# A Griffin-style block on one Trainium2 core: seven-product gate steps from output block 2 instead of 3

## The chip, the core and the metric

The kernel runs on 1 core of one Trainium2 chip. The metric is the device time of one execution in microseconds (us). Before the change it was 700.57 us, the median of 3 runs (700.04 to 700.89). The engines are called PE (TensorE matmul), PEld (its weight load), DVE (VectorE), ACT (ScalarE), POOL (GpSimd) and SP (SyncE, which here only issues DMAs).

## The reference, cut to what matters

One trunk layer over 512 positions of width 1024, in float32:

```python
h = rms_norm(x, norm_mix_g[l])
proj = h @ w_in[l]                      # conv B | conv C | conv in | q | k | v | forget | gates
y_conv = (cb * causal_dwconv(cc * cin, conv_mix_w[l])) @ w_out_conv[l]
o = forgetting_attention(q, k, v, log_f)
y_attn = o @ w_out_attn[l]
gates = jax.nn.sigmoid(g_logit + b_gate[l])
g_conv, g_attn = jnp.split(gates, 2, axis=-1)
x = x + (g_conv * y_conv + g_attn * y_attn) @ w_o[l]
...
x = x + (jax.nn.silu(a) * b) @ w_down[l]
return rms_norm(x, norm_f_g)
```

The change touches how the two gate projections (`g_logit`, 2048 columns of `proj`) are computed.

## The kernel before, in words

The activations lie transposed: 128 features on the partitions, 8 blocks of features (`KB`), 512 positions along the free axis. A float32 product is made of three passes: each weight chunk and each activation is split into a rounded high part and a low remainder, and `mm3` issues high times high, low times high and high times low, each as two matmuls of 128x256 (L290).

**The weight stream.** `stream` lists the weight chunks in the order of their use. `load` has SP fetch them up to seven chunks ahead into a ring of four buffers (`raw`); `split` then makes the high part on ACT (L259, `wh_...`) and the low part on DVE (L263, `wl_...`). There are only two `wh` and two `wl` buffers, so the high part of a chunk waits until PE is done with the chunk two places earlier. ACT and DVE each work through one fixed list of instructions in order.

**The gate and mix stage** follows the attention and runs over the output blocks j = 0 to 7. For each j it needs two gate projections (`ga`, `gb`), then the chunk `mix{j}` for the two branch outputs `yc` and `ya` (24 matmuls each), and then the merge: L946 and L947 multiply on DVE, L948 adds on POOL, L949 and L950 split the result into `mh` and `ml`. The gate projections come in two kinds:

- Plain (j = 1 and 2; those of j = 0 are done within the attention): chunks `in{20+j}` and `in{28+j}`, 48 matmuls of 128x256 each into `p_ga` and `p_gb`, evacuated by L825 on DVE and L826 on ACT.
- Steps of seven products (j = 3 to 7, `GATES`, function `seven`): a 2x2 block product (two gate columns, two feature blocks 2q and 2q+1, two halves of the positions) is made of seven products instead of eight. A step has a chunk `P{n}` (3 products of each 2x2 block) and a chunk `F{n}` (4 products of each), and covers two values of q, so that a j takes two steps: P, F, P, F, 84 matmuls on four PSUM banks named `dn`, issued by `passes` (L308). `gate_pair` combines them on ACT and DVE.

**What the steps need besides.** The `F` chunks are sums of weights, made in device memory during the attention by DMAs (`make_forms`: SP puts at L198, POOL adds at L201, in groups of two steps, one group per j). The activations need sums too. After the attention's tiles are free POOL fetches x again into `xt` (L834, four DMAs of 512 KB, one for each q). Then, for q = 0, 1 and again for q = 2, 3: ACT scales by the norm gain (L841, two instructions for each q), DVE makes four sums (L849, L850, L853, L854, each over both q), and for each q ACT makes the high part (L860, `xth`) and DVE the low part (L861, `xtl`).

**What sets the order there.** These pieces stand in the list `later`, each with the first chunk at whose split it may be put into the instruction stream and a cost in us. `run_later` puts in those that fit a budget at each split (3.0 for an `in` or `mix` chunk, 1.6 for `P`, 0.75 for `F`); `flush` puts in the rest just ahead of the products that want them.

Of the kernel before, what the change touches and what calls it, by code (L numbers as in the profile page):

```python
# [52 lines left out]
)  # L53
HELD = 2

GJ = 3
GATES = tuple(((j, q), (j, q + 1)) for j in range(GJ, KB) for q in (0, 2))

PLAIN = [(m, k) for m in (6, 7) for k in range(*PHASES[1])]
# [7 lines left out]
def block_kernel(ctx, tc, xT, vecs, wv, win, wmix, wo, wup, wst, wdp, outT):  # L67
# [13 lines left out]
    def bank(i, name):  # L81
        return ps.tile([P, S], F32, tag=f"b{i}", name=name)

    def ring(*ids):
        st = [0]

        def f(name):
            st[0] += 1
            return bank(ids[(st[0] - 1) % len(ids)], name)

        return f
# [29 lines left out]
    stream = [(f"v{kb}", wv[kb], S + H) for kb in range(KB)]  # L121
# [3 lines left out]
    def step_chunks(n):  # L125
        m = len(DOUBLES[n])
        return [(f"P{n}", wst[n, :, : 3 * m * P], 3 * m * P), (f"F{n}", n, 4 * m * P)]

    for j in range(KB):
        if j >= GJ:  # L130
            stream += step_chunks(n) + step_chunks(n + 1)
# [139 lines left out]
    def chunk(name, hl=None):  # L271

        k = chunk.n
        chunk.n += 1
        assert stream[k][0] == name
        if len(parts) == k:
            split(hl)
        return parts[k]
# [3 lines left out]
    def mm3(out, wh, wl, xh, xl, start, stop):  # L282


        n = out.shape[-1]
        cut = [slice(a, a + 2 * P) for a in range(0, n, 2 * P)] if n > 2 * P else [slice(0, n)]
        trio = ((wh, xh), (wl, xh), (wh, xl))
        for i, (w, x) in enumerate(trio):
            for c, cs in enumerate(cut):
                keep(nc.tensor.matmul(  # L290
                    out[:, cs], w, x[:, cs],
                    start=start and i == 0 and c == 0,
                    stop=stop and i == 2 and c == len(cut) - 1,
                ))
# [185 lines left out]
    def proj(idx, name, evac, bank):  # L480
        st = {}

        def half(i):
            if i == 0:
                st["w"] = chunk(f"in{idx}")
                st["p"] = bank(f"p_{name}")
            wh, wl = st["w"]
            for kb in range(4 * i, 4 * i + 4):
                ks = slice(kb * P, (kb + 1) * P)
                mm3(st["p"], wh[:, ks], wl[:, ks], xgh[:, kb, :], xgl[:, kb, :], kb == 0, kb == KB - 1)  # L490
            if i == 1:

                while len(parts) < chunk.n + 2:
                    split()
                with after_split():
                    evac(st["p"])

        return [lambda: half(0), lambda: half(1)]
# [151 lines left out]
    def run_all(fs):  # L650
        for f in fs:
            f()
# [71 lines left out]
    acc, bank_s, bank_t = ring(2, 0, 1), ring(3, 4), ring(5, 6)  # L724
# [43 lines left out]
    def seven(doubles, n0, sets, operand, goes_on=None, stays=None, done=None):  # L768


        todo, wants = [], {}
        for n, d in enumerate(doubles):
            for kind in "PF":
                prods = []
                for s_, (i, q) in enumerate(d):
                    for f, g, b, h in PROD:
                        if (f < 3) == (kind == "P"):
                            wants.setdefault(f"{kind}{n0 + n}", []).append(("q", q))
                            c = 3 * s_ + f if f < 3 else s_ + len(d) * (f - 3)
                            prods.append((c, i, operand(q, g), b, h))  # L780
                todo.append((f"{kind}{n0 + n}", prods))
        users = [{(i, b) for _, i, _, b, _ in prods} for _, prods in todo]
        for n, (name, prods) in enumerate(todo):
            wh, wl = chunk(name)
            flush(wants[name])
            before = set().union(*users[:n])
            after = set().union(*users[n + 1 :])
            out = []
            for c, i, (xh, xl), b, h in prods:
                if i not in open_:  # L790
                    flush(sets[i])
                    open_[i] = [bank(x, f"dn{n0}{i}{x}") for x in sets[i]]
                cs = slice(c * P, (c + 1) * P)
                out.append((
                    open_[i][b][:, th[h]], (i, b), wh[:, cs], wl[:, cs], xh, xl,
                    (i, b) not in before and i != goes_on, (i, b) not in after and i != stays,
                ))
            passes(out, len(out))
            if name[0] == "F":
                for i in sorted({i for _, i, *_ in prods}):  # L800
                    if (i, 0) not in after and i != stays:
                        done(i, open_.pop(i), sets[i])
            split_next()


    acc = ring(3, 4, 5, 6, 0, 1, 2, 7)
    xp = ctx.enter_context(tc.tile_pool(name="xp", bufs=1, side="right"))
    xt = xp.tile([P, KB, S], F32, tag="x1", name="xt")
    xth = xp.tile([P, KB, S], F32R, tag="x1h", name="xth")
# [12 lines left out]
    def evac_gate(idx, dst):  # L822
        def f(p):
            g = mt(f"g{idx}")
            nc.vector.tensor_mul(g, p, rb1)  # L825
            nc.scalar.activation(g, g, AF.Sigmoid, bias=col(BG + idx))  # L826
            dst.append(g)

        return f
# [32 lines left out]

        return f

    k = [c[0] for c in stream].index("mix1")
    for q in (0, 2):
        f, g = x_sums(slice(q, q + 2))
        for i in (q, q + 1):
# [14 lines left out]
    def gate_pair(j, gs):  # L883


        def done(i, banks, ids):
            p23, p45, p16, p7 = banks[0], banks[1], banks[2], banks[3][:, th[0]]
            t = {}

            def z1():  # L890
                t["z"] = mt(f"gz{j}")
                nc.scalar.activation(t["z"][:, th[0]], p16[:, th[0]], AF.Copy)
                nc.vector.tensor_add(t["z"][:, th[1]], p16[:, th[1]], t["z"][:, th[0]])

            def m1():
                gs.append(mt(f"ga{j}"))
                nc.vector.tensor_add(gs[0], p23, t["z"])

            def u3():
                t["u"] = mt(f"gu{j}")[:, : 2 * P]  # L900
                nc.vector.tensor_add(t["u"], p7, t["z"][:, th[1]])
                nc.vector.tensor_add(gs[0][:, th[1]], p45[:, th[1]], gs[0][:, th[1]])

            def m2():
                gs.append(mt(f"gb{j}"))
                nc.vector.tensor_add(
                    gs[1].rearrange(halves_of, h=2), p45.rearrange(halves_of, h=2),
                    t["u"].unsqueeze(1).to_broadcast([P, 2, 2 * P]),
                )

            def fin(n):
                def f():
                    g = gs[n]
                    nc.vector.tensor_mul(g, g, rb1)
                    nc.scalar.activation(g, g, AF.Sigmoid, bias=col(BG + 8 * n + j), scale=(1.0, -1.0)[n])

                return f

            for f, us, x in ((z1, 0.42, 2), (m1, 0.7, 0), (u3, 0.85, 3), (m2, 0.7, 1), (fin(0), 0.7, None), (fin(1), 0.7, None)):
                later.append((0, us, () if x is None else (ids[x],), f))  # L920

        return done

    for j in range(KB):
        gs = []
        if j == 0:
            evac_gate(0, gs)(gp[0])
            evac_gate(8, gs)(gp[1])
        elif j < GJ:
            run_all(proj(20 + j, f"ga{j}", evac_gate(j, gs), acc))  # L930
            run_all(proj(28 + j, f"gb{j}", evac_gate(8 + j, gs), acc))
        else:
            if j == GJ:
                acc = ring(2, 7, 3, 4)
            seven(GATES[2 * (j - GJ) : 2 * (j - GJ) + 2], 2 * (j - GJ), {j: (0, 1, 5, 6)}, gate_form, done=gate_pair(j, gs))
        wh, wl = chunk(f"mix{j}")
        yc, ya = acc(f"yc{j}"), acc(f"ya{j}")
        for pp, hh, ll, o in ((yc, ych, ycl, 0), (ya, oth, otl, 4)):
            for k in range(4):
                ks = slice((o + k) * P, (o + k + 1) * P)  # L940
                mm3(pp, wh[:, ks], wl[:, ks], hh[:, k, :], ll[:, k, :], k == 0, k == 3)
        if j >= GJ:
            split_next()
            flush()
        a, b = gs
        nc.vector.tensor_mul(a, a, yc)  # L946
        nc.vector.tensor_mul(b, b, ya)  # L947
        nc.gpsimd.tensor_add(a, a, b)  # L948
        nc.scalar.activation(mh[:, j, :], a, AF.Copy)  # L949
        nc.vector.tensor_sub(ml[:, j, :], a, mh.bitcast(F32)[:, j, :])  # L950
# [6 lines left out]
    acc = ring(0, 1, 5, 6, 3, 4, 2, 7)  # L957
# [76 lines left out]
    acc = ring(*range(6))  # L1034
# [113 lines left out]
    for ph, (j0, j1) in enumerate(PHASES):  # L1148
        if ph:
            flush()  # L1150
            acc = ring(*X)
# [212 lines left out]
```

## Time and profile before

| | |
|---|---|
| median of 3 runs | 700.57 us (700.04 to 700.89) |
| the profiled execution's own time | 700.14 us |
| span of the profile, first to last instruction | 697.9 us |
| PE busy | 689.5 us (99%) |
| DVE, ACT, POOL busy | 501.1, 344.4, 173.3 us (72%, 49%, 25%) |
| granted TensorE clock, mean | 0.997 |

The profile shows one execution. Times within it count from the span's start. A row of the timeline gives the start, the duration and in brackets the idle time of the engine before the row and who ended it; rows of the same line that follow each other are merged and counted (x4). A PE matmul's end is modelled and overlaps the next one, so a matmul's price is read from the distance between starts, or from the chain of waits, which lays pieces end to end.

### The profile page before, as it was taken

How to read it: one execution, taken by the hardware profiler on the slowest of the kernel's cores; microseconds unless marked ns; L12 is line 12 of the kernel's file. 1: busy time of each engine (PE TensorE's matmuls, PEld its weight loads, DVE VectorE, ACT ScalarE, POOL GpSimd, SP SyncE). 2: the span in 40 equal slices, each digit the busy share in tenths (PEclk: the TensorE clock that was granted, in tenths of full speed). 3: DMA queues.
4: the chain of work that ended last, by engine and by line, in shares of the span. 5: the costliest groups of instructions: out<-in, count | busy, mean ns of one | idle time of the engine just before them, and what ended most of it. 6: DMA issues, size and time to landing. Idle time of an engine off the chain costs nothing.

```text
span 697.9 us, 14608 instructions
## 1 busy us (share of the span) xinstructions
PE 689.5 (99%) x6008; PEld 688.1 (99%) x6008; DVE 501.1 (72%) x783; ACT 344.4 (49%) x546; POOL 173.3 (25%) x191
## 2 busy tenths in 40 slices
PE   9999999999999999999999999999999999999996
PEld 9999999999999999999999999999999999999995
DVE  6677877776677778754377777778674677878793
ACT  5665655545565444543344444445443344445563
POOL 4134847432200000224504214010000313221001
PEclk9999999999999999999999999999999999999998
DMA  7528989542452555587977855555647696776513
GB/s 254 161 72 274 188 196 206 116 93 86 159 165 81 177 190 177 179 301 149 216 194 168 211 130 128 151 170 166 203 126 231 139 196 157 186 169 178 153 31 121
DMA packets 52690, 116.02 MB, mean 166 GB/s; under 512 B 4960, under 2 KB 23408, under 8 KB 52624
## 3 DMA queue, kind: packets, MB, share of 16 engines
q1 hardware_dynamic: 37464, 94.17, 41.9%
q0 software_dynamic: 13920, 19.74, 17.8%
q10 hardware_dynamic: 1240, 1.19, 0.5%
q8 instruction: 47, 0.77, 0.4%
q14 instruction: 19, 0.16, 0.1%
HBM read 112.92 MB, written 33.03 MB: 209 GB/s over the span
## 4 chain that ended last, share of the span: by engine, by line
PE 97%; DMA 1%; DVE 0%; SPq 0%; ACT 0%; issue 0%; DVEq 0%; ACTq 0%
PE p_up L290 26%; PE dn L308 20%; PE p_in L290 14%; PE p_up L308 8%; PE p_wo L290 6%; PE yc L290 3%; PE ya L290 3%; PE p_q L290 2%; PE p_k L290 2%; PE p_gb L290 2%; PE p_ga L290 2%; PE o L635 2%; PE pa L454 2%; PE pb L456 1%; PE tp L618 1%; PE pdB L290 1%
## 5 line engine op out<-in xcount | busy, mean ns | idle before, releaser
L290 PE MATMUL p_up<-x1h,wl_up 128*128 128x256 f32 x536 | 104.5, 276 | 0.0
L290 PE MATMUL p_up<-x1h,wh_up 128*128 128x256 f32 x536 | 104.4, 276 | 0.0
L290 PE MATMUL p_up<-x1l,wh_up 128*128 128x256 f32 x536 | 104.4, 276 | 0.0
L259 ACT ACTIVATE wh_up<-raw_up 128x1024 fp32r<-128x1024 f32 x44 | 46.7, 1060 | 86.8 <-PE p_up L290 73.4
L290 PEld LDWEIGHTS p_up<-x1h,wl_up 128*128 128x128 f32 x536 | 80.8, 188 | 0.0
L290 PEld LDWEIGHTS p_up<-x1l,wh_up 128*128 128x128 f32 x536 | 80.7, 188 | 0.0
L290 PEld LDWEIGHTS p_up<-x1h,wh_up 128*128 128x128 f32 x536 | 80.6, 188 | 0.0
L263 DVE TENSOR_TENSOR wl_up<-raw_up,wh_up 128x1024 fp32r<-128x1024 f32 x44 | 53.8, 1223 | 20.6 <-ACT wh_up L259 20.6
L1061 POOL TENSOR_TENSOR ge<-fu,fu 128x512 f32<-128x512 f32 x11 | 17.1, 1552 | 161.6 <-DVE fu L547 150.8
L290 PE MATMUL p_in<-xgh,wh_in 128*128 128x256 f32 x288 | 56.8, 279 | 0.0
L290 PE MATMUL p_in<-xgh,wl_in 128*128 128x256 f32 x288 | 56.6, 278 | 0.0
L290 PE MATMUL p_in<-xgl,wh_in 128*128 128x256 f32 x288 | 56.5, 278 | 0.0
L201 POOL DMA_DIRECT2D f<-in_wst_dram x48 | 56.1, 1285 | 0.0
L1046 DVE TENSOR_TENSOR fz<-p_up,rb_n 128x512 f32<-128x512 f32 x44 | 30.3, 690 | 31.6 <-PE p_up L290 31.5
L263 DVE TENSOR_TENSOR wl_F<-raw_F,wh_F 128x1024 fp32r<-128x1024 f32 (+1 forms) x30 | 40.4, 1345 | 12.9 <-ACT wh_F L259 12.8
L290 PEld LDWEIGHTS p_in<-xgh,wh_in 128*128 128x128 f32 x288 | 44.7, 188 | 0.7
L259 ACT ACTIVATE wh_F<-raw_F 128x1024 fp32r<-128x1024 f32 (+1 forms) x30 | 31.5, 1051 | 27.6 <-PE dn L308 24.6
L290 PEld LDWEIGHTS p_in<-xgl,wh_in 128*128 128x128 f32 x288 | 43.7, 188 | 0.0
L290 PEld LDWEIGHTS p_in<-xgh,wl_in 128*128 128x128 f32 x288 | 43.6, 188 | 0.0
L308 PE MATMUL p_up<-x1h,wh_up 128*128 128x256 f32 x168 | 40.3, 277 | 0.0
L308 PE MATMUL p_up<-x1l,wh_up 128*128 128x256 f32 x168 | 40.2, 276 | 0.0
L263 DVE TENSOR_TENSOR wl_in<-raw_in,wh_in 128x1024 fp32r<-128x1024 f32 x26 | 34.2, 1314 | 6.7 <-ACT wh_in L259 6.5
(318 smaller groups left out, 2037.6 us busy)
## 6 DMA issues: line engine op xcount, KB each, us to landing
raw_up<-in_wup_dram SPq DMA_DIRECT2D x44, 512.0 KB, 4.4
raw_F<-f SPq DMA_DIRECT2D x29, 512.0 KB, 4.2
raw_in<-in_win_dram SPq DMA_DIRECT2D x26, 512.0 KB, 3.6
raw_P<-in_wst_dram SPq DMA_DIRECT2D x29, 384.0 KB, 4.0
f<-in_wst_dram POOLq DMA_DIRECT2D x29, 256.0 KB, 5.9
f<-in_wst_dram SPq DMA_DIRECT2D x14, 512.0 KB, 6.3
f<-in_wst_dram POOLq DMA_DIRECT2D x14, 512.0 KB, 8.1
f<-f SPq DMA_DIRECT2D x28, 256.0 KB, 4.0
```

Source lines behind the costliest of these rows:

```text
L201: return lambda: keep(nc.gpsimd.dma_start(dst, src, accum_op=ALU.add))
L259: ins = nc.scalar.activation(hi, raw, AF.Copy)
L263: ins = nc.vector.tensor_sub(lo, raw, hi.bitcast(F32))
L290: keep(nc.tensor.matmul(out[:, cs], w, x[:, cs], start=start and i == 0 and c == 0, stop=stop and i == 2 and c == len(cut) - 1,))
L308: keep(nc.tensor.matmul(out, wl if x == 1 else wh, xl if x == 2 else xh, start=opens and bk not in seen, stop=closes and bk not in left,))
L454: keep(nc.tensor.matmul(pa[t][:, :VW], xt, w[:, VB:], start=start, stop=stop))
L456: keep(nc.tensor.matmul(pb[t], xt, w[:, :VB], start=start and t % 2 == 0, stop=stop and t % 2 == 1))
L618: keep(nc.tensor.transpose(tp[:, ks], pt[:, ks], ident))
L635: keep(nc.tensor.matmul(o[:, 2 * P * e + c0 : 2 * P * (e + 1)], w, x[:, kb, c0:], start=e == 0 and kb == 0 and i == 0, stop=e == 1 and kb ...
L1046: nc.vector.tensor_mul(z, p, rb2)
L1061: keep(nc.gpsimd.tensor_mul(ge, a.rearrange(halves_of, h=2), b.rearrange(halves_of, h=2)))
```

## The change

```diff
-GJ = 3
+GJ = 2
 GATES = tuple(((j, q), (j, q + 1)) for j in range(GJ, KB) for q in (0, 2))
...
-    acc = ring(3, 4, 5, 6, 0, 1, 2, 7)
+    acc = ring(3, 4, 5, 6, 2, 7)
...
-    k = [c[0] for c in stream].index("mix1")
+    k = [c[0] for c in stream].index("mix0")
     for q in (0, 2):
         f, g = x_sums(slice(q, q + 2))
         for i in (q, q + 1):
...
             if j == GJ:
-                acc = ring(2, 7, 3, 4)
+                acc = ring(3, 4, 2, 7)
```

Output block 2 takes two steps (P0, F0, P1, F1) in place of two plain projections, so there are 12 gate steps and six groups of weight sums in place of 10 and five. The accumulators ahead of the steps go round six banks, which leaves banks 0 and 1 to the first step. The pieces of the sums of x may be put in from the chunk `mix0` on, not `mix1`. At that time the chunks `mix0` and `in21` have been split already, so the first split that takes any is that of `in29`. The chunks behind it are `mix1`, P0, F0, P1, F1, `mix2`, where they were `mix1`, `in22`, `in30`, `mix2`, P0.

**DVE, from the last mix chunk ahead of the steps to the first F chunk, before.** `p_ga`, `p_gb` are PSUM banks of the gate projections, the number behind g is the output block (8 more for the second gate).

```order
L263 TENSOR_TENSOR wl_mix2_2906<-raw_mix2_2702,wh_mix2_2905 128x1024
L861 TENSOR_TENSOR xtl_2576<-xt_2574,xth_2575 128x1024 x2
L825 TENSOR_TENSOR g2_2913<-p_ga2_2838,rb_n1_530 128x512
L263 TENSOR_TENSOR wl_P0_2968<-raw_P0_2768,wh_P0_2967 128x768
L825 TENSOR_TENSOR g10_2971<-p_gb2_2916,rb_n1_530 128x512
L946 TENSOR_TENSOR g2_2913<-g2_2913,yc2_2974 128x512
L947 TENSOR_TENSOR g10_2971<-g10_2971,ya2_2975 128x512
L263 TENSOR_TENSOR wl_F0_3052<-raw_F0_2770,wh_F0_3051 128x1024
```

Here the L861 rows are those of q = 2, 3: all sums of x are finished ahead of P0.

DVE at the same place after the change, from the row behind the low part of P0 to the low halves of q = 2, 3:

```order
L849 TENSOR_TENSOR xt_2581<-xt_2581 128x2x256
L825 TENSOR_TENSOR g9_2795<-p_gb1_2738,rb_n1_530 128x512
L850 TENSOR_TENSOR xt_2581<-xt_2581 128x2x256
L946 TENSOR_TENSOR g1_2735<-g1_2735,yc1_2798 128x512
L947 TENSOR_TENSOR g9_2795<-g9_2795,ya1_2799 128x512
L263 TENSOR_TENSOR wl_F0_2876<-raw_F0_2703,wh_F0_2875 128x1024
L950 TENSOR_TENSOR ml_2588<-g1_2735,mh_2587 128x512
L263 TENSOR_TENSOR wl_P1_2908<-raw_P1_2705,wh_P1_2907 128x768
L853 TENSOR_SCALAR xt_2581<-xt_2581 128x2x256
L854 TENSOR_SCALAR xt_2581<-xt_2581 128x2x256
L263 TENSOR_TENSOR wl_F1_2936<-raw_F1_2707,wh_F1_2935 128x1024
L861 TENSOR_TENSOR xtl_2583<-xt_2581,xth_2582 128x1024 x2
```

The sums of q = 2, 3 now stand between the splits of the step's own weights, and their low halves behind the last of these splits. On ACT the two L860 of q = 2, 3 stand likewise behind the high part of F1:

```order
L826 ACTIVATE g9_2795<-g9_2795,vec_64 128x512
L259 ACTIVATE wh_F0_2875<-raw_F0_2703 128x1024
L949 ACTIVATE mh_2587<-g1_2735 128x512
L259 ACTIVATE wh_P1_2907<-raw_P1_2705 128x768
L259 ACTIVATE wh_F1_2935<-raw_F1_2707 128x1024
L860 ACTIVATE xth_2582<-xt_2581 128x1024 x2
L259 ACTIVATE wh_mix2_2967<-raw_mix2_2721 128x1024
```

Before, ACT had them ahead of the gates of block 2 and all of P0 to F1.

**PE, the first products of P1 after the change**, with the engine that a row waits for:

```order
L308 MATMUL dn025_2855<-xgh_94,wh_P1_2907 128x256 [waits Activation_49]
L308 MATMUL dn025_2855<-xgl_95,wh_P1_2907 128x256
L308 MATMUL dn020_2853<-xgh_94,wh_P1_2907 128x256
L308 MATMUL dn020_2853<-xgl_95,wh_P1_2907 128x256
L308 MATMUL dn021_2854<-xth_2582,wh_P1_2907 128x256 [waits Activation_49]
L308 MATMUL dn021_2854<-xtl_2583,wh_P1_2907 128x256 [waits DVE_49]
L308 MATMUL dn025_2855<-xgh_94,wh_P1_2907 128x256
L308 MATMUL dn025_2855<-xgl_95,wh_P1_2907 128x256
L308 MATMUL dn020_2853<-xgh_94,wh_P1_2907 128x256
L308 MATMUL dn020_2853<-xgl_95,wh_P1_2907 128x256
L308 MATMUL dn021_2854<-xth_2582,wh_P1_2907 128x256 [waits Activation_49]
L308 MATMUL dn021_2854<-xtl_2583,wh_P1_2907 128x256 [waits DVE_49]
```

The four waits behind the first are new: the fifth and sixth product read `xth` and `xtl` of q = 2, the eleventh and twelfth those of q = 3. Before, the same products of the first P1 carried no wait of their own.

**SP after the change**, where F0, P1 and F1 follow P0 directly:

```order
L173 DMA raw_P0_2547<-in_wst_dram 128x768
L173 DMA raw_F0_2703<-f0_789 128x1024
L173 DMA raw_P1_2705<-in_wst_dram 128x768
L173 DMA raw_F1_2707<-f0_789 128x1024
L173 DMA raw_mix2_2721<-in_wmix_dram 128x1024
```

The buffers of the F chunks lie where the attention's tiles lay, so the F0 load waits for the same last DVE instruction of the attention (L647) as the four loads of `xt` on POOL. P1 and F1 wait behind it in SP's order; before, two `in` chunks stood there that needed no such buffer.

## The prediction

> **What bounds the kernel now.** First the page: busy times, then the chain that ended last.
>
> ```profile
> span 697.9 us, 14608 instructions
> PE 689.5 (99%) x6008; PEld 688.1 (99%) x6008; DVE 501.1 (72%) x783; ACT 344.4 (49%) x546; POOL 173.3 (25%) x191
> PE 97%; DMA 1%; DVE 0%; SPq 0%; ACT 0%; issue 0%; DVEq 0%; ACTq 0%
> ```
>
> PE is the bound, and it is not waiting. Whatever shortens PE's work shortens the kernel, and whatever PE has to wait for lengthens it one to one. So the change is a matter of two numbers: the matmuls it saves, and the waits it makes. Next the chain of waits in the stretch that is changed, by start and length:
>
> ```profile
> 198.62 2.72 PE yc L290 x24
> 201.34 2.72 PE ya L290 x24
> 204.06 5.44 PE p_ga L290 x48
> 209.50 5.44 PE p_gb L290 x48
> 214.94 2.72 PE yc L290 x24
> 217.66 2.72 PE ya L290 x24
> 220.38 9.52 PE dn L308 x84
> ```
>
> Without a gap PE goes from block 1 (yc, ya) to the plain gates of block 2, its yc and ya, and then the two steps of block 3. One matmul costs 9.52 / 84 = 0.113 us there.
>
> **What the change removes.** Block 2 gives up 96 matmuls (5.44 + 5.44 = 10.88 us) for the 84 of two steps (9.52 us): 10.88 - 9.52 = **1.36 us saved**, 0.19% of the time. All else must be measured against that.
>
> **What it adds: the steps' operands, earlier.** P0 now begins at 204.06, where p_ga of block 2 began. It needs the high and low halves of x's sums for q = 0, 1, and P1 those for q = 2, 3. P0 and F0 have 18 and 24 matmuls (2.04 and 2.72 us), so P1 begins at 208.8, and its fifth product, the first that reads a sum of q = 2, at 209.3. When were the last low halves ready before? ACT's and DVE's rows:
>
> ```profile
> 193.22 1.06 ACT L259 ACTIVATE wh_mix<-raw_mix 128x1024 fp32r<-128x1024 f32 x1 [2.09 <-PE p_ga L290]
> 194.19 2.56 ACT L841 ACTIVATE xt<-xt,vec 128x512 f32<-128x512 f32 x4
> 199.68 2.00 ACT L860 ACTIVATE xth<-xt 128x1024 fp32r<-128x1024 f32 x2
> 203.94 0.72 ACT L826 ACTIVATE g<-g,vec 128x512 f32<-128x512 f32 x1 [2.27 <-DVE g L825]
> 216.44 0.83 ACT L259 ACTIVATE wh_P<-raw_P 128x768 fp32r<-128x768 f32 x1
> 222.59 0.64 ACT L949 ACTIVATE mh<-g 128x512 fp32r<-128x512 f32 x1 [1.05 <-POOL g L948]
> ...
> 194.31 1.23 DVE L263 TENSOR_TENSOR wl_mix<-raw_mix,wh_mix 128x1024 fp32r<-128x1024 f32 x1 [2.17 <-ACT wh_mix L259]
> 196.16 0.69 DVE L849 TENSOR_TENSOR xt<-xt 128x512 f32<-128x512 f32 x1
> 196.95 0.69 DVE L850 TENSOR_TENSOR xt<-xt 128x512 f32<-128x512 f32 x1
> 197.68 0.69 DVE L853 SCALAR_TENSOR_TENSOR xt<-xt 128x512 f32<-128x512 f32 x1
> 198.40 0.69 DVE L854 SCALAR_TENSOR_TENSOR xt<-xt 128x512 f32<-128x512 f32 x1
> 212.81 2.36 DVE L861 TENSOR_TENSOR xtl<-xt,xth 128x1024 fp32r<-128x1024 f32 x2
> 217.30 0.96 DVE L263 TENSOR_TENSOR wl_P<-raw_P,wh_P 128x768 fp32r<-128x768 f32 x1 [1.53 <-ACT wh_P L259]
> 218.18 0.68 DVE L825 TENSOR_TENSOR g<-p_gb,rb_n 128x512 f32<-128x512 f32 x1
> 221.57 2.07 DVE L263 TENSOR_TENSOR wl_F<-raw_F,wh_F 128x1024 fp32r<-128x1024 f32 x1 [0.39 <-ACT wh_F L259]
> ```
>
> The last L861 ended at 212.81 + 2.36 = 215.2, five us ahead of the step at 220.4. Now the same operands are due at 209.3 to 210, and only one chunk of the start has been moved. So I rebuild the two in-order lists, with these durations (back to back a row costs about 0.07 less than its duration) and the order that the change gives them.
>
> *When x lands.* The four loads of xt can't go earlier, since they wait for the attention's last DVE row:
>
> ```profile
> 184.52 0.42 DVE L647 TENSOR_TENSOR otl<-oc,oth 128x256 fp32r<-128x256 f32 x1 [0.48 <-ACT oth L646]
> ...
> 185.61 2.23 POOL L834 DMA_DIRECT2D xt<-in_xT_dram  x4 [14.26 <-PE yc L290]
> 205.46 1.30 POOL L948 TENSOR_TENSOR g<-g,g 128x512 f32<-128x512 f32 x1 [15.00 <-DVE g L947]
> ...
> DMA to landing us min/median/max: 4.4/5.4/6.5
> ...
> 187.00:193.00 6.00, 6.00 (x55) 6.00 (x54) 4.10 (x4) 2.94 (x5) 2.13 (x3) 1.00 0.97 352
> 190.00:191.00 1.00, 1.00 (x12) 1.00 (x11) 1.00 (x1) 0.51 (x1) 0.46 (x1) 1.00 1.03 422
> 196.13 0.33 SPq L173 DMA_DIRECT2D raw_F<-f  x1
> ```
>
> Before, the second load (q = 1) was issued about 0.55 after the first, at 186.2, and landed at about 191.2 (5 us, between the shortest and the median); nobody needed it until 194.2. The DMA engines were full then (422 GB/s at a share of 1.03), and from 187 to 193 they moved 6 x 352 = 2.11 MB, just the four loads. Now F0, P1 and F1 (512 + 384 + 512 KB, the first of which went at 196.13) are released by the same L647 and go at 185 to 186, into the same stretch. If the two queues share evenly from 187 on, 1.05 MB of x takes 2.1 MB / 0.422 = 5.0 us, to 192.0, and with 0.8 us between the last byte and the landing (before, the bytes were through at 193, and the last landing was 187.3 + 6.5 = 193.8) q = 1 lands at **192.8**. With no contention it is 191.2; behind all of the others it is 0.5 later, 193.3. I take 192.8 and keep the ends.
>
> *First pair.* The third scale follows the landing and ends at 193.5; L849 reads only even blocks and needs no more. Then 849, 850, the merge's L950, 853, 854: 2.93 (196.16 to 199.09) + 0.62 = 3.55, to 197.1. The low part of mix1 goes to 198.2; yc of block 1 needs it at 198.6 + 0.2, so 0.5 us is left. High halves 197.2 to 199.2 on ACT, low halves to 200.6 on DVE, in time for P0. Behind them on ACT: four scales (to 201.6), the gate sigmoid (202.2), high part of P0 (203.0). On DVE: low part of P0 (to 203.9), L849 of the second pair and only then L825 of p_gb (205.2).
>
> *First stall.* The sigmoid behind it ends at 205.9, and the high part of F0 at 207.0. PE wants it at 204.06 + 2.04 = 206.1: about **1.0 us**. DVE does 850, 946, 947 meanwhile, and from 207.1 the low part of F0, which takes 2.07 beside POOL's L948 (as the row at 221.57): to 209.1. PE wants it 16 matmuls (1.8) after 207.1: **0.3**.
>
> *Second stall.* F0 ends on PE at 210.1, and P1's four first products at 210.6. But L949 on ACT waits for POOL's L948 (1.30, to 208.5) and ends at 209.1, the high part of P1 at 209.9; DVE does L950 and the low part of P1 (to 210.9), then 853 and 854 (to 212.3). Only then can ACT make the high halves of q = 2 (213.4) and q = 3 (214.3), and DVE, behind the low part of F1 (213.4), the low halves: 214.6 and 215.8. PE waits from 210.6 for 213.4, **2.8**; after one product for 214.6, **1.1**; five products on for 215.8, **0.5**.
>
> Sum: 1.0 + 0.3 + 2.8 + 1.1 + 0.5 = 5.7 of waits, less 1.36 = **+4.4 us**. What stands behind is as before: F1's parts are ready, mix2 has its 2.7 us of F1 as cover, and each later block repeats block 3. With x at 191.2 all moves 1.6 us earlier, +2.8; at 193.3 it is +4.9. Were x there at once, the chain would start behind the low part of in29 and the scales, some 2 us earlier: +2.4. None of these ends is a gain.
>
> *What costs nothing.* The sixth group of weight sums adds three POOL adds in the attention:
>
> ```profile
> L201 POOL DMA_DIRECT2D f<-in_wst_dram x48 | 56.1, 1285 | 0.0
> POOL pp L602 <- DVE m L601: 24.2, 13, 2.9
> ```
>
> POOL sits idle for its softmax rows for 24.2 us there, which covers 3 x 1.285 = 3.9 us; without that cover, 3.9 us is the most it costs. Six accumulators instead of eight put block 1's p_ga and p_gb into banks 5 and 6, which the step itself opens; L825 frees them at 201.2 and 205.2, ahead of the products that open them (at 204.06 and in F0, from 207.0). No cost, at most the 0.1 of one product.
>
> **Does the stall slow the clock too?** PE's last matmuls and the clock after them:
>
> ```profile
> 689.81 0.75 PE L1246 MATMUL warm_to<-gl,gh 128*128 128x256 f32 x5
> 690.40 0.61 PE L344 MATMUL pb_n<-ident,rc_n 128*128 128x128 f32 x4
> 693.00:693.50 0.50, 0.00 (x0) 0.00 (x0) 0.47 (x2) 0.00 (x0) 0.00 (x0) 1.00 0.44 150
> 693.50:694.00 0.50, 0.00 (x0) 0.00 (x0) 0.00 (x0) 0.00 (x0) 0.00 (x0) 0.94 1.00 342
> 694.00:694.50 0.50, 0.00 (x0) 0.00 (x0) 0.00 (x0) 0.00 (x0) 0.00 (x0) 0.50 1.09 381
> 1.05 3.89 PE L111 MATMUL warm<-ones 128*128 128x128 f32 x18 [1.05 <-DVE ones L103]
> ```
>
> PE ended at 691.0 and the granted clock fell to half at about 693.9, 2.9 us later. My longest wait is 2.8, and the three of the second stall, 4.4 us, have only six matmuls between them: near enough to be a rival. If half speed then lasts as long as the 3.7 us for which the warm-up products run at the start, it costs half of that, about 1.9 us. The Trainium skill, "TensorE: Matmul & The Clock Gate", Part 1, says that the clock is halved after an idle window of about 3.4 us, in a window that runs freely; by that rule a wait of 2.8 alone would not do it and the sum would stay at +4.4. The 2.9 us here are shorter than its window, so the trace doesn't settle it.
>
> **The rivals.**
> 1. *The clock falls to half in the second stall.* +4.4 + 1.9 = +6.3 us. Against it: each wait by itself is short of 2.9.
> 2. *The operands come in time* (faster): the saved matmuls stay, -1.36 us, 0.2% at once. It decides at the low half of q = 3: if it is done by 210 and not at 215.8, PE never waits. For it speaks that DVE is busy for 72% only; against it that the order is fixed and that even x landing at once leaves 3.8 us of waits.
> 3. *The change does little on balance*: waits of about 1.4 us eat the gain. The chain would have to be 4 us shorter than its rows.
> 4. *The attention pays too*: the three POOL adds and their DMAs hold up a softmax row, up to 3.9 us on top, +8.3. Against it POOL's idle time above.
>
> **How the numbers follow.** The profiled execution took 700.14 us, 2.2 more than its span; the median of the runs is 700.57, 0.43 more. By the profiled execution the forecast is 704.5, by the median 705.0; I give **705.0**. Chances: forecast 0.68 (703.0 to 705.7), the clock 0.17 (706.9), operands in time 0.05 (699.2), little on balance 0.03, the attention 0.07 (up to 708.9). The range 702.9 to 707.3 takes in the forecast with its ends and the clock, and leaves out the rest. A measurement tells about 0.2% (1.4 us) from no change: slower 0.92, same 0.05, faster 0.03; the operands' case, whose gain of 0.19% lies at that bound, is shared between the last two.
>
> **What would show it.** In the changed profile: no p_ga or p_gb of block 2, 12 matmuls fewer; PE waiting in P1 for L860 and L861, longest about 2.8 us, and for the parts of F0; F0, P1 and F1 loads issued by 186; the second scale pair on ACT idle until about 192.8; yc of block 2 at about 214.9 + 4.4 = 219.3. If PE shows no idle time in P1, the chain is wrong; if it does and the time is longer than the waits say, look at the clock.

## The result and the profile after

| | before | after |
|---|---|---|
| median | 700.57 us, with the runs beside after 700.6 (700.04 to 700.89) | 710.91 us (710.03 to 711.23, 4 runs) |
| ratio, 95% interval | | 1.0149 (1.0137 to 1.0161) |
| profiled execution, span | 700.14, 697.9 us | 711.05, 709.3 us |
| granted clock, mean | 0.997 | 0.990 |

The change costs 10.3 us where 4.4 were forecast. The page first: twelve matmuls fewer, and yet PE is busy for 4.6 us longer than before. Work that got smaller but takes longer points at the clock.

```profile
span 709.3 us, 14610 instructions
PE 694.1 (98%) x5996; PEld 691.6 (98%) x5996; DVE 503.9 (71%) x790; ACT 346.0 (49%) x549; POOL 177.3 (25%) x194
PE 93%; DMA 2%; DVE 2%; ACT 1%; issue 1%; POOL 0%; SPq 0%; DVEq 0%; ACTq 0%; POOLq 0%
```

PE's waits after (engine, tile and line that waited, then who was waited for; total, times, longest). L860 and L861 in P1 are there as forecast. New is the wait ahead of block 1's yc; the two waits in F0 are missing.

```profile
PE dn L308 <- ACT xth L860: 2.7, 1, 2.7
PE yc L290 <- DVE wl_mix L263: 2.0, 1, 2.0
...
PE dn L308 <- DVE xtl L861: 0.7, 1, 0.7
...
PE dn L308 <- ACT wh_P L259: 0.5, 1, 0.5
PE yc L290 <- ACT wh_mix L259: 0.2, 1, 0.2
```

They come to 6.1 us, close to the forecast's 5.7, but partly by luck: 2.7 of them (ahead of yc and for wh_P) were not forecast, and 1.8 of the forecast (F0's two and P1's third) are missing. The waits alone don't explain 10.3. PE's idle time in the profile grew by 6.8 us (15.2 against 8.4), of which these waits and a program start that is 0.6 later make up 6.7; the other 4.6 are busy time. The chain of waits after shows where the rest is: PE leaves the chain at the xt load, comes back 33 us later at P1, and then 37 matmuls take 6.76 us, 0.183 each. Block 3's 84 take 9.52 again, 0.113 each.

```profile
182.87 2.80 PE yc L290 x24
...
186.26 9.08 DMA xt<-in_xT_dram
...
217.84 1.22 DVE xtl L861
...
219.10 6.76 PE dn L308 x37
225.86 2.72 PE yc L290 x24
...
231.30 9.52 PE dn L308 x84
```

The same stretch cut into pieces of 3.41 us that begin and end where the granted clock changed (start and end, length, PE busy and its matmuls, PEld, DVE, ACT, POOL, then the granted clock, DMA share, GB/s):

```profile
200.10:203.51 3.41, 1.54 (x13) 1.54 (x14) 3.36 (x4) 2.63 (x4) 0.00 (x0) 1.00 0.16 23
203.51:206.92 3.41, 3.41 (x19) 3.41 (x18) 1.63 (x3) 3.17 (x5) 0.00 (x0) 0.50 0.32 93
206.92:210.33 3.41, 3.41 (x32) 3.41 (x31) 3.41 (x6) 1.42 (x2) 0.00 (x0) 1.00 0.02 5
...
213.75:217.16 3.41, 0.88 (x6) 0.53 (x4) 3.33 (x5) 2.01 (x3) 0.00 (x0) 1.00 0.59 204
217.16:220.58 3.42, 2.06 (x8) 1.77 (x9) 3.02 (x3) 1.58 (x2) 0.00 (x0) 0.50 0.41 109
220.58:223.99 3.41, 3.41 (x18) 3.41 (x18) 1.22 (x1) 1.06 (x1) 0.00 (x0) 0.50 0.51 201
```

Behind each wait the clock stands at 0.50, once for one piece and once for two. A full piece then holds 18 or 19 matmuls instead of 32.

Last the head of the chain, ACT's, DVE's and POOL's rows, and the landing of the four xt loads, 4.4/5.4/6.5 us before:

```profile
195.37 2.58 ACT L841 ACTIVATE xt<-xt,vec 128x512 f32<-128x512 f32 x4 [5.42 <-DMA xt<-in_xT_dram]
213.02 0.63 ACT L949 ACTIVATE mh<-g 128x512 fp32r<-128x512 f32 x1 [2.44 <-POOL g L948]
...
197.37 0.69 DVE L849 TENSOR_TENSOR xt<-xt 128x512 f32<-128x512 f32 x1 [5.20 <-ACT xt L841]
210.62 1.23 DVE L263 TENSOR_TENSOR wl_F<-raw_F,wh_F 128x1024 fp32r<-128x1024 f32 x1
...
210.75 2.24 POOL L948 TENSOR_TENSOR g<-g,g 128x512 f32<-128x512 f32 x1 [19.66 <-DVE g L947]
...
DMA to landing us min/median/max: 9.1/10.4/12.4
```

ACT and DVE both stand idle for over 5 us waiting for x. L849 starts at 197.37; the forecast had it at 193.5. What the two queues moved (q0 is POOL's queue with xt, q1 is SP's; packets, MB, share of the 16 engines), before from 187 to 190, and after from 187 to 190 (the first two rows) and from 190 to 193 (the last two):

```profile
q0 software_dynamic: 233, 0.89, 89.3%
```

```profile
q1 hardware_dynamic: 208, 0.70, 82.0%
q0 software_dynamic: 3, 0.01, 2.0%
...
q1 hardware_dynamic: 175, 0.59, 52.1%
q0 software_dynamic: 148, 0.58, 48.6%
```

In the first three us POOL's queue moved almost nothing beside F0, P1 and F1; only then did the two share evenly. The load of q = 1, issued at 186.90, landed 9.7 us later, at 196.6.

### The profile page after: what moved, and what is told of

It reads as the page before. It is cut to its first block, busy times and chain, and to the rows that moved or that the text cites. A ratio compares the mean times of both kernels' runs of the same rounds, so it can differ in the third digit from the quotient of the medians.

```text
span 709.3 us, 14610 instructions
## 1 busy us (share of the span) xinstructions
PE 694.1 (98%) x5996; PEld 691.6 (98%) x5996; DVE 503.9 (71%) x790; ACT 346.0 (49%) x549; POOL 177.3 (25%) x194
## 4 chain that ended last, share of the span: by engine, by line
PE 93%; DMA 2%; DVE 2%; ACT 1%; issue 1%; POOL 0%; SPq 0%; DVEq 0%; ACTq 0%; POOLq 0%
PE p_up L290 26%; PE dn L308 21%; PE p_in L290 14%; PE p_up L308 8%; PE p_wo L290 6%; PE yc L290 3%; PE ya L290 2%; PE p_q L290 2%; PE p_k L290 2%; PE o L635 2%; PE pa L454 1%; PE pb L456 1%; DMA xt<-in_xT_dram 1%; PE tp L618 1%; PE pdB L290 1%; PE pdA L290 1%
## 5 line engine op out<-in xcount | busy, mean ns | idle before, releaser
L201 POOL DMA_DIRECT2D f<-in_wst_dram x51 | 60.4, 1315 | 0.1
L263 DVE TENSOR_TENSOR wl_F<-raw_F,wh_F 128x1024 fp32r<-128x1024 f32 (+1 forms) x32 | 42.8, 1338 | 12.8 <-ACT wh_F L259 12.8
L259 ACT ACTIVATE wh_F<-raw_F 128x1024 fp32r<-128x1024 f32 (+1 forms) x32 | 33.6, 1050 | 26.9 <-PE dn L308 24.6
L259 ACT ACTIVATE wh_P<-raw_P 128x768 fp32r<-128x768 f32 (+1 forms) x32 | 26.6, 832 | 28.9 <-PE dn L308 23.6
```

What stands on the lines that cost most here:

```text
L201: return lambda: keep(nc.gpsimd.dma_start(dst, src, accum_op=ALU.add))
L259: ins = nc.scalar.activation(hi, raw, AF.Copy)
L263: ins = nc.vector.tensor_sub(lo, raw, hi.bitcast(F32))
```

## The experiments

**Theory A**: the loss is made of three things: P1's operands stand behind a fixed list of work on ACT and DVE (the forecast), x lands late because of SP's loads in the other queue, and the clock falls behind the waits. The **rivals** that the runs had to rule out: the low clock costs nothing because PE would wait anyway (B); the landing doesn't matter (E); POOL's queue is slow here by itself (F); the early sums or the six banks cost by themselves (G). Ratios are to the kernel before on the same chip.

**1. Fill the waits.** Extra matmuls that nothing reads stand where PE waited.

```diff
+            if name == "P1":
+                fill_pe(3, 28)
...
+        if j == 1:
+            fill_pe(0, 17)
```

> The changed kernel with 45 extra matmuls whose results nothing reads: 17 of 256 columns ahead of yc1 of block 1 and 28 ahead of the step P1, where TensorE waits 2.2 us and 2.7 + 0.7 + 2.0 us in the trace after. They work only in time that is a wait there, so they add nothing but keep TensorE from standing still. Theory A (the waits' second price is the clock: the granted clock stands at 0.5 for some 3.4 us after the first wait and some 6.8 us after the second, and 37 matmuls of P1 and F1 then take 6.76 us where 37 x 0.113 = 4.19 are due): the clock stays near 1.0 and the kernel takes 708.0 to 709.0 us, 2 to 3 us less than the changed kernel's 710.9. Rival B (the low clock of the records costs nothing by itself, or what follows waits for the x pieces anyway): 710.9 within 0.4, the waits longer by what TensorE saves. Rival C (the fills come after the waits and are paid): 712 or more.

709.36 us (708.84 to 710.15), ratio 1.0130 (1.0115 to 1.0145): 1.55 less than the change, though PE has 45 matmuls more to do. The clock stays at 1.00 in every slice. The gain is smaller than the 2 to 3 expected. Its waits, and the first product with the low half of q = 2:

```profile
PE dn L308 <- ACT wh_F L259: 1.1, 1, 1.1
...
PE dn L308 <- DVE xtl L863: 1.0, 2, 0.9
PE dn L308 <- ACT xth L862: 0.4, 1, 0.4
PE yc L290 <- DVE wl_mix L263: 0.3, 1, 0.3
```

```profile
218.30 0.38 PE L308 MATMUL dn<-xtl,wh_P 128*128 128x256 f32 x1 [0.87 <-DVE xtl L863]
```

With PE at full speed F0 has the forecast's wait for its high part (1.1, forecast 1.0). In the changed kernel the first low stretch hid it: PE reached F0 later. That wait takes nothing from the gain: the low half of q = 2, which ends the chain through ACT and DVE, is ready 182.2 us after the first k projection, in the changed kernel 182.4. What is won lies behind it. From its first product to block 2's yc (at 223.36) it is 5.1 us here and 6.8 in the changed kernel, so 1.7 are won and not the 2.6 that the second low stretch costs (below), in part because at full speed PE comes to the low half of q = 3 before it is ready and stands once more. So B holds for the first stretch and falls for the second.

**2. xt on SP's queue, ahead of F0.**

```diff
-        nc.gpsimd.dma_start(xt[:, 2 * q : 2 * q + 2, :], xT[:, 2 * q : 2 * q + 2, :])
+        nc.sync.dma_start(xt[:, 2 * q : 2 * q + 2, :], xT[:, 2 * q : 2 * q + 2, :])
```

> The changed kernel with the four loads of xt issued by SP, ahead of the F0, P1 and F1 loads in SP's queue, instead of by POOL. Theory A (xt's loads start about 3 us late and land at 195.4 because they stand in POOL's queue beside SP's; the second scale pair and all sums hang on them): the first xt load lands within 4 to 6 us of its issue, near 190, the waits ahead of P1 come to 1 to 2 us, TensorE's block 2 ends 5 to 8 us earlier than in the changed kernel, and the time is 703.5 us if the clock holds and 705.5 if it falls after the wait of yc1. Rival D (F0, P1 and F1, put behind xt, then land late in their turn): wh_P or wh_F waits of 2 us or more appear and the time stays above 708. Rival E (the landing isn't what matters, since the scales and sums on ACT and DVE stand behind the mix1 split): the landing moves, the waits of P1 stay above 4 us and the time stays within 1 us of 710.9.

705.46 us (704.71 to 706.15), ratio 1.0073 (1.0058 to 1.0088), the time that A expected with the clock falling: **5.4 us of the loss are the landing**. The waits are not those that it expected: 3.9 us are left in P1, not 1 to 2, and the clock falls behind these and not behind block 1's. xt lands 5.7/6.1/6.5 us from issue, and the wait ahead of yc is gone:

```profile
PE dn L308 <- ACT xth L860: 2.7, 1, 2.7
...
PE dn L308 <- DVE xtl L861: 0.9, 1, 0.9
...
PE dn L308 <- ACT wh_P L259: 0.3, 1, 0.3
```

Those are the forecast's second stall (2.8 and 1.1). Behind it the clock falls for two pieces:

```profile
209.58:212.99 3.41, 0.61 (x3) 0.20 (x2) 3.38 (x5) 2.01 (x3) 0.00 (x0) 1.00 0.28 111
212.99:216.40 3.41, 2.67 (x12) 2.67 (x13) 1.82 (x2) 1.10 (x2) 0.00 (x0) 0.50 0.79 250
216.40:219.82 3.42, 3.42 (x18) 3.42 (x17) 1.23 (x1) 0.33 (x1) 0.00 (x0) 0.50 0.33 106
```

D and E are out.

**3. Hold back the F loads.**

```diff
+            if tag == "rg" and len(parts) < first_rg:
+                return
```

> The changed kernel with the loads of the first F and P weights held back until mix1 is split, so that xt's loads have the DMA engines to themselves as in the kernel before; xt stays on POOL's queue. Theory A: xt lands in 4.4 to 6.5 us from issue as before, the time is 703.6 us if the clock holds and 705.6 if it falls. Rival F (POOL's queue itself is slow here, whatever runs beside it): the first load still takes about 9 us and the time stays near 710.9. Rival E (landing not what matters): landing moves, time within 1 us of 710.9.

710.43 us, ratio 1.0147 (1.0131 to 1.0162), with nothing learnt about F: the edit held none of these loads back, and SP issued F0 and F1 at 185.70 and 186.55, as in the changed kernel. It serves as a repeat of the change.

**4. Only the early sums, in the kernel before.**

```diff
-    k = [c[0] for c in stream].index("mix1")
+    k = [c[0] for c in stream].index("mix0")
```

> The kernel before with only the third part of the change: the sums of x are begun from the first mix chunk on, gate steps of seven products still from block 3 and eight accumulating banks. Theory A (the early sums cost nothing where nothing waits for them): 700.6 us within 0.4, no wait of TensorE above 1.0 us between 176 and 250. Rival G (the early scales on ACT and sums on DVE delay the gates and splits of blocks 0 and 1 at any place): 702 or more, with waits for wh_mix, wl_mix or an accumulating bank in blocks 1 and 2.

700.13 us, ratio 0.9998 (0.9989 to 1.0008), no wait of PE in the stretch. The early sums cost nothing by themselves.

**5. Only the six banks, in the kernel before.**

```diff
-    acc = ring(3, 4, 5, 6, 0, 1, 2, 7)
+    acc = ring(3, 4, 5, 6, 2, 7)
...
-                acc = ring(2, 7, 3, 4)
+                acc = ring(3, 4, 2, 7)
```

> The kernel before with only the second part of the change: six accumulating banks in front of the first gate step (3, 4, 5, 6, 2, 7) in place of eight, and 3, 4, 2, 7 after it; gate steps of seven from block 3 and sums from the second mix chunk on as before. Theory A (banks 0 and 1 were not needed there): 700.5 us within 0.4 and no wait of TensorE above 1.0 between 176 and 250. Rival G (an accumulating bank comes round too early and TensorE waits for the gate product L825 or the products L946 and L947): 702 or more.

700.11 us, ratio 0.9998 (0.9989 to 1.0007), no wait there either. G is out: it is the earlier steps that cost.

**6. The change without the early sums** (the first two parts, `index("mix1")` kept).

> The change without its third part: gate steps of seven products from output block 2 and six banks, the sums of x begun from the second mix chunk on as before. What each theory gives: by the waits alone (wh_P1 0.9, xth of q=2 5.6, xtl 1.2 and 0.5 in P1, none before yc1; 8.0 us less the 1.36 of twelve matmuls) 706.9 us; with the granted clock at half for some 6.8 us after that wait, about 709.4 (theory A). The landing of xt plays no part here, since the sums stand behind it anyway. If the early sums are what makes the changed kernel slow (they let the mix1 split stand behind the late xt), this one is faster than the changed kernel's 710.9; if they are a help (rival), it is slower, 712 or more.

708.75 us (708.63 to 708.96), ratio 1.0115 (1.0099 to 1.0132): 2.2 us *faster* than the whole change (706.9 were expected by the waits alone, 709.4 with the half clock). The longest wait in P1 is 5.2 us, but block 1 doesn't wait at all; the clock is at half for two pieces behind the wait, from 214.73 on. Its longest wait, and the pieces around it:

```profile
PE dn L308 <- ACT xth L860: 5.2, 1, 5.2
```

```profile
207.90:211.32 3.42, 1.97 (x15) 1.56 (x14) 1.83 (x4) 2.83 (x4) 0.00 (x0) 1.00 0.72 206
211.32:214.73 3.41, 0.00 (x0) 0.00 (x0) 3.17 (x5) 0.07 (x1) 0.00 (x0) 1.00 0.50 145
214.73:218.14 3.41, 1.70 (x6) 1.41 (x7) 2.36 (x2) 1.93 (x2) 0.00 (x0) 0.50 0.60 225
```

So in the whole change the early sums do harm: they put block 1's own split of mix1 behind a load that is late. With xt on time (run 2) they are worth up to 708.75 - 705.46 = 3.3 us, a little less if run 6 too had x on time: its L849 waits 0.4 us for x.

**7. xt on SP, and P1's wait filled with 30 matmuls.** Runs 2 and 7 differ only by the fill.

> The changed kernel with xt's loads on SP, as in the run that took 705.5 us, and 30 extra matmuls of 256 columns, read by nothing, ahead of the step P1, where TensorE stood 2.7 us for xth. Nothing else is moved, so this separates the wait from the clock. Theory A (the clock at half from 213 to 219.6 costs some 2.5 to 3 us after the wait of 3.9): clock near 1.0 in every slice and 702.5 to 703.3 us. Rival B (the matmuls at half clock hide behind work that ACT and DVE still have to do): 705.0 to 705.9 as without the fills.

704.31 us (703.74 to 704.41), ratio 1.0051 (1.0036 to 1.0066), the clock at 1.00 throughout; 1.15 us less than run 2, less than the 2.5 to 3 expected. In the two profiled executions the gain is 2.4 us from the first low half in P1 to block 2's yc (213.73 to 221.08 in run 2, 214.21 to 219.17 here). The medians differ by half of that; run 2's times spread over 1.4 us, and the profile shows only one of them. Why the rest is missing in the medians stays open.

**8. The same with 20 matmuls.**

> As the run with 30 extra matmuls ahead of P1 and xt on SP, but with 20 (2.3 us), so that they are sure to end before xth of q=2 lands at 212.5: TensorE still waits some 0.5 for xth and 0.9 for xtl. Theory A: no slice below 0.9 of the clock, and the time 0 to 0.4 below that run's 704.3, so about 704.0; the clock's price is then 705.46 less this. If a stand of 1.4 us in pieces is enough to lower the clock (rival H), the profile shows 0.5 for 3.4 us or more and 705.5 is back.

705.66 us (705.09 to 705.98), ratio 1.0075 (1.0061 to 1.0088). This went against A and for H: waits of 0.8 and 0.9 us were enough.

```profile
PE dn L308 <- DVE xtl L863: 1.0, 2, 0.9
PE dn L308 <- ACT xth L862: 0.8, 1, 0.8
```

```profile
208.36:211.78 3.42, 3.42 (x32) 3.42 (x31) 2.81 (x4) 2.18 (x3) 0.00 (x0) 1.00 0.75 253
211.78:215.19 3.41, 1.74 (x12) 1.23 (x10) 3.41 (x4) 2.01 (x2) 0.00 (x0) 1.00 0.33 78
215.19:218.60 3.41, 3.24 (x15) 3.15 (x15) 1.40 (x2) 1.06 (x1) 0.00 (x0) 0.50 0.61 232
```

PE was busy for 1.74 of the 3.41 us ahead of the fall, 51%. It is not the longest wait that sets it off: a single one of 1.3 us in run 10 and of 1.1 in run 11 left the clock at 1.00.

**9. F0, P1 and F1 on POOL's queue, behind xt.** F0 is then issued at 190.96.

```diff
+                eng = nc.gpsimd if nm in ("F0", "P1", "F1") else nc.sync
```

> The changed kernel with the loads of F0, P1 and F1 issued by POOL behind the four xt loads and block 0's gate addition, instead of by SP; xt stays in POOL's queue. Theory A (POOL's queue moves late only because SP's loads stand beside it): the first xt load lands 4.4 us after its issue and the last 6.5, as in the kernel before; F0 lands near 195 to 197; the waits are those of the run with xt on SP and the time is 705 to 706.5 us. Rival F (POOL's queue starts late after something in this kernel, whatever SP does): first landing still near 9 us and 709 or more.

706.31 us (705.17 to 707.46), ratio 1.0081 (1.0066 to 1.0097), and the landing of the kernel before is back:

```profile
DMA to landing us min/median/max: 4.2/5.3/6.4
```

F is out: POOL's queue is not slow, it starts late beside SP's loads. F0 landed at 198.8, later than the 195 to 197 expected, and PE did not wait for it.

**10. Both pairs' sums ahead of block 1's splits**, with xt on SP.

```diff
-        later.append((k, 1.4, (("q", q),), f))
-        later.append((k, 1.5, (("q", q),), g))
+        later.append((k, 0.7, (("q", q),), f))
+        later.append((k, 0.75, (("q", q),), g))
...
-            later.append((k + 1, 1.25, (("q", i),), x_split(i)))
-        k += 2
+            later.append((k + 3, 0.7, (("q", i),), x_split(i)))
+        k += 0
```

> The changed kernel with xt's loads on SP and the pieces of x's sums handed to the planner with lower costs (0.70 and 0.75 for the sums, 0.7 for the splits, the second pair's from the first mix chunk on as well), so that both pairs' sums go ahead of block 1's splits. If P1's operands are what is late (theory A), no wait for xth or xtl is left; one of about 1.7 us for wh_F ahead of F0 and 0.3 for wl_F come in its place: 700.8 us if the clock holds, 702 to 703.5 if it falls after a wait of 1.7. Rival E (ACT and DVE have more to do ahead of P1 than fits, in whatever order): waits of 4 us in all, 704 or more.

701.30 us, ratio 1.0010 (1.0001 to 1.0019). That is 0.5 us above what was expected with the clock holding. P1 no longer waits; one wait is left, and the clock stays at 1.00:

```profile
PE dn L308 <- ACT wh_F L259: 1.3, 1, 1.3
```

Of the 10.3 us of loss 9.5 are gone (0.76 are left), by the order of the work and the queue of four loads alone.

**11 and 12. The second pair's splits behind F0's** (`k + 5` for q = 2, 3, and a cost of 0.70 in place of 0.75), and then also the additions of blocks 0 and 1 on DVE:

```diff
-        nc.gpsimd.tensor_add(a, a, b)
+        (nc.vector if j < 2 else nc.gpsimd).tensor_add(a, a, b)
```

> The run that took 701.3 us (xt on SP, sums of both pairs early), with the splits of x's second pair handed to the planner two chunks later, so that they stand behind the split of F0 and not ahead of it. Theory A (DVE's row of work ahead of F0 and P1 is what is left): the wait for wh_F of 1.3 us goes and one of about 1.3 us for xtl takes its place ahead of P1's products; 700.3 to 701.3 us, the clock at 1.0. Rival: two waits, 702 or more.

> As the run before it in this call, and the additions of the two gated products of blocks 0 and 1 on DVE (0.69 us each there) in place of POOL (1.30 each, during which a split of 1024 columns on DVE took 2.2 us instead of 1.2). Theory A (DVE's time is the last limit): 0.6 us less waiting, so 699.6 to 700.4 us, at or below the kernel before, and never under it by more than the 1.36 us of the twelve matmuls. Rival (DVE has no room for them): above 701.

700.30 us, ratio 1.0002 (0.9993 to 1.0010), with one wait of 1.1 for xtl; and 699.91 us, ratio 0.9991 (0.9982 to 1.0000), with one of 0.4:

```profile
PE dn L308 <- DVE xtl L861: 0.4, 1, 0.4
```

In run 12 block 2's yc comes 215.02 - 182.92 = 32.10 us after block 0's, before 214.94 - 182.24 = 32.70: 0.6 of the 1.36 us are kept. That is a gain at the edge of what the runs can tell from none.

## Why the prediction was wrong

The direction was right, and so was the fixed order on ACT and DVE as a cause. The size was not: 705.0 forecast, range to 707.3, measured 710.9. The landing of x was taken too early, and the clock, held as a rival, came on top. By the profile block 2's yc stands at 225.86, forecast 214.94 + 4.4 = 219.34, 6.5 later. Of this:

| term | us | from |
|---|---|---|
| x later than taken | 3.2 | L849 at 197.37, less 0.63 of start, against 193.5 |
| POOL's addition in block 1, 0.9 longer than taken, less 0.3 won ahead of it | 0.6 | xtl of q = 2 ends at 219.06, against 214.6 + 0.63 + 3.2 |
| half clock in P1 and F1 | 2.6 | 6.76 for 37 matmuls, against 37 x 0.113 = 4.18 |
| the last wait, hidden by slow matmuls | -0.5 | forecast xtl of q = 3, not among the waits |
| start of the program | 0.6 | block 0's yc at 182.87, against 182.24 |

Without the last term they come to 5.9 us, which is what the median lies above the forecast. The half clock by itself (2.6 - 0.5, so 707.1) would have stayed inside the range; the late x took the time out of it. The last term is no effect of the change: the profiles of the other runs have this start anywhere between 182.2 and 182.9, and from the first k projection (36.02 before, 36.68 after) to block 0's yc it is 146.06 before and 146.03 after:

```profile
36.68 0.49 PE L290 MATMUL p_k<-xgh,wh_in 128*128 128x256 f32 x2
182.71 0.45 PE L290 MATMUL yc<-ych,wh_mix 128*128 128x256 f32 x2
```

By its own steps:

- *What the change removes*, 1.36: right. 5996 matmuls after, 6008 before. (5.7 - 1.36 is 4.34, rounded up to 4.4.)
- ***When x lands* failed.** The step was "If the two queues share evenly from 187 on", giving 192.8 for q = 1. It landed at 196.6, 196.0 less the later start. The queues did not share: POOL's moved 0.01 MB of 0.71 in the first three us, and the two together moved 1.88 MB from 187 to 193, where 6 x 0.422 = 2.53 were reckoned with. The far end, 193.3, was also summed wrongly: F0, P1 and F1 (1.44 MB) ahead of 1.05 MB of x take 5.9 us at 0.422, which gives 193.7. Even that is 2.3 us too early: the step took bytes for the only thing that a load waits for. Runs 2 and 9 take the collision away in two ways and win 5.4 and 4.6 us.
- *First pair*: the 0.5 us that were left for mix1 were eaten by that landing, and a wait of 2.0 + 0.2 stood there instead. Run 2, with x on time, has none.
- *First stall*, 1.0 + 0.3: right in its cause (1.1 in run 1; the 0.3 for the low part shows in no run), hidden in the changed kernel by the half clock ahead of it.
- *Second stall*, 2.8, 1.1, 0.5: right to within 0.4 us for the first two (2.7 and 0.7, and 2.7 and 0.9 in run 2); the third is hidden by the half clock. One row was priced on the wrong side: the forecast charged DVE for sharing with POOL (2.07 for wl_F and 1.30 for L948), but wl_F came 0.13 us first and took 1.23, and L948 took 2.24. The Trainium skill, "SBUF — State Buffer", section "SBUF: two separate sides", says that DVE and GpSimd share a port pair as a lock, and that whichever starts first has it for its whole instruction. The rows agree: 2.24 - 1.30 = 0.94 us on the side that came second; held back until wl_F's end at 211.85, it would be 1.10.
- *What costs nothing*: right. The sums and the banks alone are at 0.9998 each, and the stretch of the attention with the sixth group is as long as before.
- *Rival 1, the clock*, at a chance of 0.17 with 1.9 us, came true, and twice: once hidden, as run 1 shows, and once at 2.6 us in this profile. It was held too unlikely because each wait was measured against 2.9 us by itself. The Trainium skill, "TensorE: Matmul & The Clock Gate", Part 1, has the clock fall after an idle window of about 3.4 us. The length of its window agrees with every stretch here (3.41 us or twice that); that the window must be idle does not: 51% busy was low enough in run 8.

With x on time most of the forecast's other steps hold. In run 2's profile block 2's yc stands at 221.08; for x at its near end the forecast gave 219.34 - 1.6 = 217.7. Of the 3.3 us between, some 2.7 lie in P1 and F1 (7.35 us from the first low half on, against 4.18 + 0.5) and some 0.7 ahead of them (that low half is ready at 213.68, against 214.6 - 1.6 = 213.0). This profile is at +5.9 us, the median of run 2 at +5.2, and the fill of run 7 takes only 1.15 off the median; so how much of the median is the clock stays open.

## What to carry to other kernels

Two queues whose loads become due at the same moment need not share evenly: here POOL's started about three us behind SP's, and its second load landed later than a sum by bytes alone gives, even with the others put first. Moving such a load into the other queue, ahead of the others, is a cheap test. Waits of PE that stand close together should be added up before the clock is judged: in run 8 two of under 1 us each were enough to halve it for 3.4 us. A saving that needs its operands earlier is first of all a question of order on the helper engines: here 10.3 us of loss went away, to a time at or just under the one before, with nearly the same work in another order.

## What the runs showed of the hardware

- **The clock goes by what a piece of time holds, not by the longest wait.** Its changes lie 3.41 us or a multiple of it apart within a run. Pieces in which PE was busy for 0.00, 0.61, 0.88, 1.54 and 1.74 of 3.41 us were followed by half clock; one of 1.97 (run 6) was not. One of 1.75, in run 3, was not either (the first row below), so among these pieces the border lies near a half. The busy time alone does not decide everywhere: at the end of run 4 a piece with 2.18 us (the last row) was followed by half clock too. Its matmuls are other ones, 8 of the 20 with a single column of output; which measure the clock goes by stays open.

```profile
213.02:216.43 3.41, 1.75 (x14) 1.35 (x12) 2.47 (x4) 2.31 (x3) 0.17 (x1) 1.00 0.80 266
216.43:219.85 3.42, 0.93 (x5) 0.73 (x6) 3.42 (x4) 2.00 (x2) 0.00 (x0) 1.00 0.15 52
...
688.90:692.31 3.41, 2.18 (x20) 1.98 (x18) 0.89 (x3) 1.20 (x4) 0.68 (x1) 1.00 0.31 110
```

- At half clock, pieces busy for 1.70, 2.06 and 2.67 us were followed by another at half, those of 3.24 and more by full speed.
- **POOL's queue starts late beside SP's loads.** Issued at 186.26 beside SP's loads, it moved 3 packets from 187 to 190; issued at 185.61 alone, in the kernel before, 233, and at 186.19 alone, in run 9, 178. DVE's rows at that time are the same in run 9 as in the changed kernel, so they alone are not the cause. What holds the start up wasn't tried.
